# A decoder trunk in three-pass fp32r: up units as 512-column passes split around the products, a thirteenth Strassen block, and a pinned order for the first unit

## The chip, the cores and the metric

The kernel runs on one core of one Trainium2 chip. The metric is device time in microseconds of one execution; the time before is 938.76 us, the median of three runs (938.64 to 938.79). The core has five engines with a queue each: PE (TensorE, matrix products into PSUM), DVE (VectorE), ACT (ScalarE), POOL (GpSimd) and SP (SyncE), the last two here mostly issuing DMAs. Each queue runs in its own order; semaphores tie them together.

## The reference

Two decoder layers on 256 tokens of width 1024, in float32. Each layer has two sub-layers with a norm on both sides; the first has three branches (sliding-window attention, a gated recurrence, a causal pool), merged by gates. The change touches the second:

```python
mix = merged @ w_out[l]
h = h + rms_norm(mix, norm_mix_post[l])
m = rms_norm(h, norm_mlp_pre[l])
y = jnp.square(jax.nn.relu(m @ w_mlp_up[l])) @ w_mlp_down[l]     # 1024 -> 4096 -> 1024
h = h + rms_norm(y, norm_mlp_post[l])
```

and the start of the first layer, where the first 512 columns of the projection (keys and values) are computed from the normed input.

## The kernel before

**Products in three passes.** PE multiplies float32 operands in the type fp32r. To keep the precision, every operand is split into a high part (ScalarE writes a copy in fp32r, L99) and a low part (VectorE subtracts the copy, L100). A product is then high x high + high x low + low x high, three matmuls into the same PSUM bank (`mm3`, L106 to L109). Every weight passes through this: SP loads a unit of 128 x 1024 ("raw", seven buffers), ScalarE and VectorE make "wh" and "wl" (eight buffers each, shared with the other weight forms named below).

**Two forms of a product with the features on PSUM's free side.** `w_unit` (L373) makes one up unit: 256 hidden columns by 256 tokens, in two halves n of 128 hidden columns, each of 8 chunks x 3 matmuls with 256 moving columns, into one bank. `w_unit2`, used in the input projection, stores high and low features side by side, so that one matmul of 512 moving columns takes the weights' high part against both (L360), and a matmul of 256 takes the low part against the high features (L362); ScalarE copies the second half of the bank out, and VectorE adds the first half to it (`joined`).

**The block loop of the MLP** (`for j in range(nstr)`). The 4096 hidden columns make 16 blocks of 256. For the first 12 blocks the down product is done by Strassen's scheme: seven products (`down`, 21 matmuls) in place of eight (24 matmuls), accumulated over the blocks in seven PSUM banks of the eight. A block needs its weights in combined forms: "dh/dl" and "bh/bl" are splits of what the host laid out as differences, "sh/sl" are splits of two sums of weights. The sums of pairs ("dsum") are made in DRAM by accumulating DMAs (`make_sums`, issued at the steps SUM_AT of the first sub-layer); two further sums ("t") are made the same way for the blocks in FOUR, and by two VectorE adds (L917, L918) for the others. `hidden_forms` makes the forms of the hidden values ("sm", "xf"; L886 to L889). One round j of the loop: up unit j + 3 (the first round has two), forms for block j + 1, the seven products of block j. The last four blocks are plain (`plain`, 24 matmuls per block): block 12 alone, then 13 to 15 together (LAST), ordered by tokens and halves so that the norm behind can start early.

**The start.** PE runs six warm-up matmuls and three smaller ones (L136, L140). `first_features` transposes four chunks of the input at a time and writes their high and low parts, scaled by the gain; `kv_first` runs the key and value unit: four weight units, for each two token tiles of six matmuls, with the transposes of the other parts of the input placed between them. A scheduler orders each engine's instructions by when it thinks they can run, and by priority: `tc.high_priority` moves work ahead. The order on each queue is then fixed.

Of the kernel before, what the change touches and what calls it, by code (L numbers as in the profile page):

```python
# [18 lines left out]
T = 256  # L19
P = 128  # L20
# [6 lines left out]
WARM = (6, 3)  # L27
# [29 lines left out]

KV_ORDER = ((0, 0), (0, 1), (1, 0), (1, 1), (2, 0), (2, 1), (3, 0), (3, 1))
# [8 lines left out]
def trunk(ctx, tc, x, wts, rgw, par, gpost, eye, ctab, out):  # L67
# [28 lines left out]

    def split(hi, lo, src, scale=None):
        if scale is None:
            A.activation(hi, src, AF.Copy)  # L99
            V.tensor_tensor(out=lo, in0=src, in1=hi.bitcast(F32), op=ALU.subtract)  # L100
        else:
            A.activation(hi, src, AF.Copy, scale=scale)
            V.scalar_tensor_tensor(out=lo, in0=src, scalar=scale, in1=hi.bitcast(F32),
                                   op0=ALU.mult, op1=ALU.subtract)

    def mm3(o, lh, ll, rh, rl, start, stop, **kw):  # L106
        PE.matmul(o, lh, rh, start=start, stop=False, **kw)  # L107
        PE.matmul(o, lh, rl, start=False, stop=False, **kw)  # L108
        PE.matmul(o, ll, rh, start=False, stop=stop, **kw)  # L109
# [25 lines left out]
    for i in range(WARM[0]):  # L135
        PE.matmul(wps[:], warm[:, 0:P], warm[:], start=True, stop=True)  # L136

    def warm_up(n):
        for i in range(n):
            PE.matmul(wps[:, 0:256], warm[:, 0:P], idt[:].bitcast(BF16), start=True, stop=True)  # L140
# [49 lines left out]

    def split_to(n):
        while st["split"] < min(n, NHU):
            i = st["split"]
            load_to(i + 1)
            r = raw_t.pop(i)
            wh = his.tile([P, HU_COLS], F32R, tag="wh", name=f"wh{i}")
            wl = los.tile([P, HU_COLS], F32R, tag="wl", name=f"wl{i}")
            parts = 2 if i in fine else 1
            for k in range(parts):
                sl = slice(k * HU_COLS // parts, (k + 1) * HU_COLS // parts)  # L200
                split(wh[:, sl], wl[:, sl], r[:, sl])
            hu_t[i] = (wh, wl)
            st["split"] += 1
        load_to(n + NRAW - 1)
# [59 lines left out]
    def first_features(tt, part):  # L264

        tsl = slice(tt * P, (tt + 1) * P)
        ps = bank([P, 4, P])
        for c in range(4):
            PE.transpose(ps[:, c, :], h[:, tt, (4 * part + c) * P:(4 * part + c + 1) * P], ident)
        for c0 in (0, 2):  # L270
            for c in range(c0, c0 + 2):
                gain = prm[:, 0, PG_PRE + 4 * part + c:PG_PRE + 4 * part + c + 1]
                A.activation(uh[:, 4 * part + c, tsl], ps[:, c, :], AF.Copy, scale=gain)
                V.scalar_tensor_tensor(out=ul[:, 4 * part + c, tsl], in0=ps[:, c, :], scalar=gain,
                                       in1=uh[:, 4 * part + c, tsl].bitcast(F32), op0=ALU.mult, op1=ALU.subtract)
            yield

# [95 lines left out]
    def w_unit(hus, xh, xl):  # L373

        ps = bank([P, 2, T])
        for n in range(2):
            for i, (wh, wl) in enumerate(hus):
                a = wh.rearrange("p (k n) -> p k n", k=4)
                b = wl.rearrange("p (k n) -> p k n", k=4)
                for k in range(4):  # L380
                    c = 4 * i + k
                    mm3(ps[:, n, :], a[:, k, n * P:(n + 1) * P], b[:, k, n * P:(n + 1) * P],
                        xh[:, c, :], xl[:, c, :], c == 0, c == 7)
        return ps

    def s_hu(ps, hu, xh, xl, c0, tt, start, stop):
        wh, wl = hu
        a = wh.rearrange("p (k n) -> p k n", k=2)
        b = wl.rearrange("p (k n) -> p k n", k=2)
        for k in range(2):  # L390
            tsl = slice(tt * P, (tt + 1) * P)
            mm3(ps, xh[:, c0 + k, tsl], xl[:, c0 + k, tsl], a[:, k, :], b[:, k, :],
                start and k == 0, stop and k == 1)
# [53 lines left out]
    fa = first_features(0, 0)  # L447
    next(fa)
    warm_up(WARM[1])
    split_to(1)  # L450
    next(fa)
    load_to(CST)
    nc.sync.dma_start(cst[:], ctab)

    for l in range(L):
# [14 lines left out]
        def kv_first():  # L470

            pss = [bank([P, 512]) for _ in range(2)]
            for n, (i, tt) in enumerate(KV_ORDER):
                if tt == 0:
                    hk, = take(1)
                    hks.append(hk)
                s_hu(pss[tt][:], hks[i], uh, ul, 2 * i, tt, i == 0, i == 3)
                for t_, part in X_AFTER.get(n, ()):
                    hp(list)(first_features(t_, part))
# [390 lines left out]

        def up(j):
# [58 lines left out]
        def down(j, part):  # L930
            f = forms[j]
            w1, w4, w2, w3 = wforms[j]
            lo_, up_ = slice(0, 512), slice(512, 1024)

            for p, blk, w, cs in ((1, 2, w1, up_), (3, 6, w1, lo_), (2, 0, w4, lo_), (7, 5, w2, lo_), (5, 3, w2, up_),
                                  (6, 4, w3, lo_), (4, 1, w3, up_))[part]:
# [15 lines left out]
        for j in range(nstr):  # L952
            if j % 2 and j + 3 < nstr:
                load_sums(j + 3)
            for i in range(UPS[j]):
                up(nup)
# [6 lines left out]
                down(j, slice(0, 7) if UPS[j] == 1 else (slice(0, 4), slice(4, 7))[i])  # L963
# [30 lines left out]
        def last_rows(hus):  # L994
# [28 lines left out]
            V.tensor_tensor(out=rest[1][1][:], in0=tgt[1][1][:], in1=rest[1][1][:], op=ALU.add)  # L1023
# [10 lines left out]
        for j in range(nstr, NBLK - LAST):  # L1034
            if j not in hids:
                hidden_split(j)
            hus = take(2)
            ahead()
            for tt in range(2):
                for nh in range(2):  # L1040
                    if tgt[tt][nh] is None:
                        tgt[tt][nh] = bank([P, 512], nm="pr")
                    plain(j, hus, tt, nh)
            if j == nstr:
                rest = drain()
# [7 lines left out]
        for tt in range(2):  # L1053
# [3 lines left out]
            for nh in range(2):  # L1057
                for b in range(LAST):
# [50 lines left out]
def _layout(i):  # L1109
    qc = np.concatenate([np.arange(hd * 64, hd * 64 + 64) for hd in _HEADS])  # L1110
    units, rg, par, gp = [], [], [], []
    for l in range(L):
# [17 lines left out]
        up = _w_units(i["w_mlp_up"][l]).reshape(NBLK, 2, P, HU_COLS)  # L1130
# [47 lines left out]
```

## Time and profile before

| what | value |
|---|---|
| median of three runs | 938.76 us |
| the profiled execution | 938.37 us, of which the span on the core is 936.6 us |
| block loop and plain block 12, layer 0 (timeline of PE) | from 319.63 us, with ups 4 to 15; plain blocks from 446.34 us |
| splits of weights on VectorE (L100, wl) | 296 rows, 325.1 us |
| splits of weights on ScalarE (L99, wh) | 296 rows, 281.5 us |
| DMA | 217.30 MB, mean 232 GB/s |

How to read the profile: the page gives for each engine its busy time and share, then the span in 40 slices, the DMA queues, the chain of work that ended last (followed back from the last instruction to what released it), and groups of equal instructions with busy time and mean duration. A timeline row is: start in us, duration in us, engine, line, operation, what it writes <- what it reads, shape, count, and in brackets the idle time before it and who ended it. Matmuls overlap each other, so the time that one costs is the distance to the next start, not its duration.

### The profile page before, as it was taken

Reading aid. Unit: us, or ns where it says so; the run is one execution under the profiler, and the core shown is the slowest. Engines: PE = TensorE matmul, PEld = TensorE weight load, DVE = VectorE, ACT = ScalarE, POOL = GpSimd, SP = SyncE. Lnnn points to the kernel's source line nnn. Section 1 sums busy time; section 2 is a strip of 40 time slices with the busy share of each in tenths; the row PEclk is TensorE's granted clock in tenths of the full one; section 3 lists DMA queues with packets and bytes.
Section 4 is the critical chain, followed back from the end, with each engine's and each line's share of the span. In section 5 each row is a group of like instructions: output and inputs, shape, how many; then the busy total and the mean of one; then the engine's idle time right before and its main releaser. Section 6 shows DMA issues by size and latency. Waiting matters only on the chain.

```text
span 936.6 us, 14405 instructions
## 1 busy us (share of the span) xinstructions
PE 928.2 (99%) x5183; PEld 798.0 (85%) x5183; DVE 765.8 (82%) x1401; ACT 643.1 (69%) x1106; POOL 39.2 (4%) x44
## 2 busy tenths in 40 slices
PE   9999999999999999999999999999999999999997
PEld 6888977888888999999888888888888889999986
DVE  6978997989668798888786788788995597898884
ACT  7765765798637787677575665668894478777661
POOL 0001101001000000000000101010000000000000
PEclk9999999999999999999999999999999999999999
DMA  9898898968864767766469988978796467767631
GB/s 350 290 308 244 272 259 246 307 212 224 245 203 151 242 200 264 245 224 214 147 209 308 263 233 248 300 212 273 227 265 207 157 225 225 259 213 237 197 130 45
DMA packets 65496, 217.30 MB, mean 232 GB/s; under 512 B 7056, under 2 KB 7696, under 8 KB 65040
## 3 DMA queue, kind: packets, MB, share of 16 engines
q1 hardware_dynamic: 56160, 199.30, 61.0%
q0 software_dynamic: 8832, 16.78, 11.5%
q8 instruction: 40, 0.66, 0.3%
q14 instruction: 32, 0.26, 0.1%
q10 hardware_dynamic: 432, 0.30, 0.1%
HBM read 215.30 MB, written 34.60 MB: 267 GB/s over the span
## 4 chain that ended last, share of the span: by engine, by line
PE 99%; DMA 1%; DVE 0%; SPq 0%; ACT 0%; DVEq 0%; issue 0%
PE ps L107 18%; PE ps L109 18%; PE ps L108 18%; PE ps L360 9%; PE ps L400 7%; PE pr L107 6%; PE pr L108 6%; PE pr L109 6%; PE ps L362 5%; PE ps L534 1%; PE ps L582 1%; PE ps L571 1%; PE ps L283 1%; DMA h<-x 1%; PE ps L514 0%; PE ps L761 0%
## 5 line engine op out<-in xcount | busy, mean ns | idle before, releaser
L100 DVE TENSOR_TENSOR wl<-raw,wh 128x1024 fp32r<-128x1024 f32 (+1 forms) x296 | 325.1, 1120 | 61.9 <-ACT wh L99 52.5
L99 ACT ACTIVATE wh<-raw 128x1024 fp32r<-128x1024 f32 (+1 forms) x296 | 281.5, 983 | 116.3 <-PE ps L109 54.4
L107 PE MATMUL ps<-m,wh 128*128 128x256 f32 x448 | 126.8, 283 | 0.0
L109 PE MATMUL ps<-m,wl 128*128 128x256 f32 x448 | 126.8, 283 | 0.0
L108 PE MATMUL ps<-m,wh 128*128 128x256 f32 x448 | 126.8, 283 | 0.0
L360 PE MATMUL ps<-u,wh 128*128 128x512 f32 x384 | 96.9, 394 | 0.0
L107 PE MATMUL ps<-wh,u 128*128 128x512 f32 x224 | 87.7, 392 | 0.0
L109 PE MATMUL ps<-wh,u 128*128 128x512 f32 x224 | 87.4, 390 | 0.0
L108 PE MATMUL ps<-wl,u 128*128 128x512 f32 x224 | 87.4, 390 | 0.0
L108 PEld LDWEIGHTS ps<-m,wh 128*128 128x128 f32 x448 | 85.9, 192 | 1.0
L107 PEld LDWEIGHTS ps<-m,wh 128*128 128x128 f32 x448 | 85.9, 192 | 1.0
L109 PEld LDWEIGHTS ps<-m,wl 128*128 128x128 f32 x448 | 85.9, 192 | 0.0
L360 PEld LDWEIGHTS ps<-u,wh 128*128 128x128 f32 x384 | 69.4, 189 | 13.6 <-issue 0.7
L99 ACT ACTIVATE sh<-dsum 128x1024 fp32r<-128x1024 f32 x24 | 25.4, 1057 | 48.1 <-PE ps L108 48.1
L362 PEld LDWEIGHTS ps<-u,wl 128*128 128x128 f32 x384 | 52.4, 190 | 3.8
L362 PE MATMUL ps<-u,wl 128*128 128x256 f32 x384 | 53.5, 282 | 0.0
L107 PEld LDWEIGHTS ps<-wh,u 128*128 128x128 f32 x224 | 42.1, 188 | 9.7 <-issue 0.7
L109 PEld LDWEIGHTS ps<-wh,u 128*128 128x128 f32 x224 | 42.0, 188 | 8.8
L108 PEld LDWEIGHTS ps<-wl,u 128*128 128x128 f32 x224 | 42.1, 188 | 8.5 <-DVE wl L100 0.3
L169 POOL DMA_DIRECT2D sums<-wts x24 | 26.1, 1087 | 547.5 <-DMA sums<-wts 535.3
L100 DVE TENSOR_TENSOR sl<-dsum,sh 128x1024 fp32r<-128x1024 f32 x24 | 29.4, 1224 | 20.5 <-ACT sh L99 20.5
L553 ACT ACTIVATE pr<-ps,s 128x128 f32<-128x128 f32 (+1 forms) x64 | 25.9, 431 | 20.2 <-DVE s L544 20.2
(263 smaller groups left out, 2046.2 us busy)
## 6 DMA issues: line engine op xcount, KB each, us to landing
raw<-wts SPq DMA_DIRECT2D x291, 512.0 KB, 4.7
sums<-wts SPq DMA_DIRECT2D x24, 512.0 KB, 6.9
sums<-wts POOLq DMA_DIRECT2D x24, 512.0 KB, 8.6
dsum<-sums SPq DMA_DIRECT2D x12, 1024.0 KB, 6.4
raw<-wts SPq DMA_DIRECT2D x26, 256.0 KB, 3.5
sums<-wts SPq DMA_DIRECT2D x16, 256.0 KB, 6.9
sums<-sums POOLq DMA_DIRECT2D x16, 256.0 KB, 5.2
t<-sums SPq DMA_DIRECT2D x8, 512.0 KB, 4.4
```

Of the source, the lines that this page charges most:

```text
L99: A.activation(hi, src, AF.Copy)
L100: V.tensor_tensor(out=lo, in0=src, in1=hi.bitcast(F32), op=ALU.subtract)
L107: PE.matmul(o, lh, rh, start=start, stop=False, **kw)
L108: PE.matmul(o, lh, rl, start=False, stop=False, **kw)
L109: PE.matmul(o, ll, rh, start=False, stop=stop, **kw)
L169: nc.gpsimd.dma_start(t, u1[:, 0:512].unsqueeze(1).to_broadcast([P, 2, 512]), accum_op=ALU.add)
L283: PE.transpose(banks[c // 4][:, c % 4, :], src[c // 4][:, (c % 4) * P:(c % 4 + 1) * P], ident)
L360: PE.matmul(ps[:], ws[0][c], x2[:, :, c, :], start=c == 0, stop=False)
L362: PE.matmul(ps[:, 0, :], ws[1][c], x2[:, 0, c, :], start=False, stop=c == 7)
L400: PE.matmul(o, xx[:, c, tsl], ww[c], start=(n == 0 and c == 0), stop=(n == 2 and c == 7))
L534: PE.matmul(sc[hd // hp][:, hd % hp, :], qT[a, j // 2][rows, j % 2, blk * P:(blk + 1) * P], kTs[0][rows, a, 0:w], start=True, stop=True)
L553: A.activation(pr[:, j, :], sc[i][:, j, :], AF.Exp, bias=negm[:, hd:hd + 1], accum_out=sums[:, hd:hd + 1])
```

## The change

It has three parts.

1. In both layers, up units 5 to 15 (WIDE) take the form of `w_unit2`: `up_wide(j, n, hu)` makes one half n by eight matmuls of 512 columns and eight of 256, then a ScalarE copy, a VectorE add (both at high priority), relu and square. The first three of the block's seven products stand between the two halves, the other four behind the second. The host lays the up weights out so that a weight unit holds one half n whole; the old `w_unit` follows. The order of products 2 and 3 is exchanged.
2. 13 blocks go by Strassen's scheme, 3 are plain; every round has one up unit. FOUR has six blocks now, 0, 1 and 2 among them. The sums of pairs 10 to 12 are issued in rounds 0, 2 and 4 of the block loop (SUM_LATE).
3. Everything up to the end of the key and value unit keeps the order in which it is written (`pin`). The code there is written out step by step; `first_features` uses two banks of two chunks; small warm-up matmuls ("fill") stand between the first matmuls: 7 and 4 at the very start in place of 6 and 3, nine more in the first unit.

The core of the diff:

```diff
-WARM = (6, 3)
+WARM = (7, 4, (2, 0, 1, 3, 0, 0), 3)
-PLAIN = 4
+PLAIN = 3
-UPS = (2, 1, 1, 1, 1, 1, 1, 1, 1, 1, 1, 1)
+UPS = (1,) * 13
+WIDE = tuple(range(5, 16))
-SUM_AT = tuple(range(1, 25, 2))
-FOUR = (1, 4, 7, 10)
+SUM_AT = tuple(range(1, 21, 2))
+SUM_LATE = {3: 10, 5: 11, 7: 12}
+FOUR = (0, 1, 2, 4, 6, 8)
...
+    def pin(ins):
+        if pinned[0]:
+            tc.keep_in_program_order(ins)
...
+            unit(())
+            part(0, 0, WARM[2])
+            fb = first_features(1, 0)
+            next(fb)
+            warm_up(WARM[3])
+            next(fb)
+            unit((None, None, fb))
+            part(0, 1)
...
+        def up_wide(j, n, hu):
+            if n == 0:
+                zs[j] = ttile([P, 2, T], nm="z")
+            a, b = [w.rearrange("p (k n) -> p k n", k=8) for w in hu]
+            ps = bank([P, 2, T])
+            for c in range(8):
+                PE.matmul(ps[:], a[:, c, :], u2[:, :, c, :], start=c == 0, stop=False)
+            for c in range(8):
+                PE.matmul(ps[:, 0, :], b[:, c, :], u2[:, 0, c, :], start=False, stop=c == 7)
+            t = ttile([P, T], nm="jt")
+            with tc.high_priority(HP):
+                A.activation(t[:], ps[:, 1, :], AF.Copy)
+                V.tensor_tensor(out=t[:], in0=ps[:, 0, :], in1=t[:], op=ALU.add)
+            A.activation(t[:], t[:], AF.Relu)
+            A.activation(zs[j][:, n, :], t[:], AF.Square)
...
-                up(nup)
+                parts = slice(0, 7) if UPS[j] == 1 else (slice(0, 4), slice(4, 7))[i]
+                if nup in WIDE:
+                    hus = take(2)
+                    up_wide(nup, 0, hus[0])
+                    mid = parts.start + 3
+                    down(j, slice(parts.start, mid))
+                    up_wide(nup, 1, hus[1])
+                    parts = slice(mid, parts.stop)
+                else:
+                    up(nup)
+                if nup in SUM_LATE:
+                    make_sums(l, SUM_LATE[nup])
...
-        for j in range(nstr, NBLK - LAST):
...
+        rest = drain()
```

**PE in a round of the block loop.** Before, the last matmuls of an up unit (ps) and the first products (pr):

```order
L107 MATMUL ps<-m,wh_4127 128x256
L108 MATMUL ps<-m,wh_4127 128x256
L109 MATMUL ps<-m,wl_4128 128x256
L107 MATMUL pr<-dh,xf 128x512
L108 MATMUL pr<-dl,xf 128x512
```

Of the change, a whole first pass, three products, and the start of the second pass:

```order
L925 MATMUL ps<-m,wh_4062 128x512 x8
L927 MATMUL ps<-m,wl_4063 128x256 x8
L117 MATMUL pr<-dh,xf 128x512
L119 MATMUL pr<-dl,xf 128x512
L121 MATMUL pr<-dh,xf 128x512
L117 MATMUL pr<-bh,xf 128x512
L119 MATMUL pr<-bl,xf 128x512
L121 MATMUL pr<-bh,xf 128x512
L117 MATMUL pr<-dh,xf 128x512
L119 MATMUL pr<-dl,xf 128x512
L121 MATMUL pr<-dh,xf 128x512
L925 MATMUL ps<-m,wh_4066 128x512 x8
```

48 matmuls ahead of 21 have become 16, nine, 16 and twelve.

**VectorE in such a round**, where it makes the sums itself (t). Before:

```order
L100 TENSOR_TENSOR wl_4124<-raw_3991,wh_4123 128x1024
L100 TENSOR_TENSOR wl_4128<-raw_4011,wh_4127 128x1024
L100 TENSOR_TENSOR sl<-dsum,sh 128x1024
L100 TENSOR_TENSOR sl<-t_4100,sh 128x1024
L100 TENSOR_TENSOR bl<-raw_3897,bh 128x512
L886 TENSOR_TENSOR sm<-z 128x128
```

Of the change:

```order
L931 TENSOR_TENSOR jt<-ps,jt 128x256
L110 TENSOR_TENSOR wl_4401<-raw_4293,wh_4400 128x1024
L110 TENSOR_TENSOR sl<-dsum,sh 128x1024
L110 TENSOR_TENSOR sl<-t_4373,sh 128x1024
L110 TENSOR_TENSOR dl<-raw_4295,dh 128x1024
L931 TENSOR_TENSOR jt<-ps,jt 128x256
L110 TENSOR_TENSOR bl<-raw_4185,bh 128x512
L952 TENSOR_TENSOR sm<-z 128x128
```

Two adds (jt, L931) have come in, the first between two splits of up weights, the second behind the split of dl. ScalarE's rows around the second pass's copy (jt, L930), of the change:

```order
L109 ACTIVATE sh<-t_4373 128x1024
L109 ACTIVATE dh<-raw_4295 128x1024
L930 ACTIVATE jt<-ps 128x256
L109 ACTIVATE bh<-raw_4185 128x512
L109 ACTIVATE wh_4509<-raw_4384 128x1024
L932 ACTIVATE jt<-jt 128x256
```

The copy stands behind dh, and the relu (L932) two rows behind the copy.

**PE at the start**, from the first transposes of the input (h) on. Before:

```order
L107 MATMUL ps<-wh_136,u 128x512
L108 MATMUL ps<-wl_137,u 128x512
L269 MATMUL ps<-idt,h 128x128 x4
L109 MATMUL ps<-wh_136,u 128x512
L107 MATMUL ps<-wh_136,u 128x512
```

Of the change (buffer numbers kept; L153 are fills):

```order
L117 MATMUL ps_160<-wh0_135,u_114 128x512
L153 LDWEIGHTS warm_95
L153 MATMUL ps_99<-warm_95 128x256
L153 LDWEIGHTS warm_95
L153 MATMUL ps_99<-warm_95 128x256
L119 MATMUL ps_160<-wl0_136,u_114 128x512
L121 MATMUL ps_160<-wh0_135,u_114 128x512
L153 LDWEIGHTS warm_95
L153 MATMUL ps_99<-warm_95 128x256
L117 MATMUL ps_160<-wh0_135,u_114 128x512
```

The transposes of the second token tile (L288) have moved behind all six matmuls of the first unit, and fills have come between these. On VectorE the low parts of the features (u) stand there in another place too. Before:

```order
L100 TENSOR_TENSOR wl0_137<-raw0_116,wh0_136 128x512
L274 SCALAR_TENSOR_TENSOR u_113<-ps_124,prm_87,u_113 128x128
L100 TENSOR_TENSOR wl0_137<-raw0_116,wh0_136 128x512
L274 SCALAR_TENSOR_TENSOR u_113<-ps_124,prm_87,u_113 128x128
L274 SCALAR_TENSOR_TENSOR u_113<-ps_167,prm_87,u_113 128x128
```

Of the change:

```order
L110 TENSOR_TENSOR wl0_136<-raw0_117,wh0_135 128x512
L296 SCALAR_TENSOR_TENSOR u_114<-ps_125,prm_87,u_114 128x128 x2
L110 TENSOR_TENSOR wl0_136<-raw0_117,wh0_135 128x512
L296 SCALAR_TENSOR_TENSOR u_114<-ps_126,prm_87,u_114 128x128 x2
L296 SCALAR_TENSOR_TENSOR u_114<-ps_176,prm_87,u_114 128x128 x2
```

Two rows of u, not one, now stand ahead of the second half of wl0.

More of the change, by code (lines that the diff above doesn't have):

```diff
@@ L189, in load_to, with split_parts @@
             st["load"] += 1
+    def split_parts():
+        i = st["split"]
+        load_to(i + 1)
+        r = raw_t.pop(i)
+        wh = his.tile([P, HU_COLS], F32R, tag="wh", name=f"wh{i}")
+        wl = los.tile([P, HU_COLS], F32R, tag="wl", name=f"wl{i}")
+        hu_t[i] = (wh, wl)
+        st["split"] += 1
+        parts = 2 if i in fine else 1
+        for k in range(parts):
+            sl = slice(k * HU_COLS // parts, (k + 1) * HU_COLS // parts)
+            split(wh[:, sl], wl[:, sl], r[:, sl])
+            yield
     def split_to(n):
         while st["split"] < min(n, NHU):
[L193 to L203, printed above, removed]
+            list(split_parts())
         load_to(n + NRAW - 1)
@@ L392, in s_hu @@
             mm3(ps, xh[:, c0 + k, tsl], xl[:, c0 + k, tsl], a[:, k, :], b[:, k, :],
-                start and k == 0, stop and k == 1)
+                start and k == 0, stop and k == 1, fill=fill[3 * k:3 * k + 3])
     def by_pass(o, xh, xl, wh, wl, tt, mid=None):
@@ L472, in kv_first, with part, unit @@
             pss = [bank([P, 512]) for _ in range(2)]
[L473 to L479, printed above, removed]
+            def part(i, tt, *fill):
+                s_hu(pss[tt][:], hks[i], uh, ul, 2 * i, tt, i == 0, i == 3, *fill)
+            def unit(steps):
+                w = split_parts()
+                for f in steps:
+                    next(f if f else w, None)
+                hks.append(take(1)[0])
+            unit(())
[6 more added lines that the diff above has]
+            part(0, 1)
+            fa = first_features(0, 1)
+            next(fa)
+            part(1, 0)
+            fb = first_features(1, 1)
+            next(fb)
+            part(1, 1)
+            unit((fa, None, None, fa, fb))
+            part(2, 0)
+            part(2, 1)
+            unit((None, None, fb))
+            part(3, 0)
+            part(3, 1)
+            pinned[0] = False
             for tt in range(2):
```

93 lines of the change are left out of this document (46 added, 47 removed).

## The prediction

> **What bounds the kernel.** I read the page first: busy shares, the clock line, and the chain of work that ended last.
>
> ```profile
> span 936.6 us, 14405 instructions
> PE 928.2 (99%) x5183; PEld 798.0 (85%) x5183; DVE 765.8 (82%) x1401; ACT 643.1 (69%) x1106; POOL 39.2 (4%) x44
> PEclk9999999999999999999999999999999999999999
> PE 99%; DMA 1%; DVE 0%; SPq 0%; ACT 0%; DVEq 0%; issue 0%
> ```
>
> The chain is matrix work almost from end to end, and the granted clock shows no throttling. So a saved microsecond of PE is a microsecond of time, as long as nothing else becomes late. VectorE is the next engine, at 82% on average, but the average hides the stage that the change touches; there I look at one round.
>
> The timeline of PE gives the price of one round of the block loop in layer 0: an up unit of 48 matmuls, then 21 matmuls of seven Strassen products.
>
> ```profile
> 372.38 0.28 PE L107 MATMUL ps<-m,wh 128*128 128x256 f32 x1
> 372.49 0.28 PE L108 MATMUL ps<-m,wh 128*128 128x256 f32 x1
> ...
> 378.01 0.28 PE L109 MATMUL ps<-m,wl 128*128 128x256 f32 x1
> 378.13 0.40 PE L107 MATMUL pr<-dh,xf 128*128 128x512 f32 x1
> ...
> 380.21 0.39 PE L107 MATMUL pr<-sh,xf 128*128 128x512 f32 x1
> ...
> 382.96 0.28 PE L107 MATMUL ps<-m,wh 128*128 128x256 f32 x1
> ```
>
> Durations overlap, so I use starts. The up unit takes 378.13 - 372.38 = 5.75 us (0.12 per matmul of 256 columns), the seven products 382.96 - 378.13 = 4.83, their first three (nine matmuls) 380.21 - 378.13 = 2.08. A round is 10.58 us and PE never pauses in it.
>
> **Part 1, the wide up units.** The same arithmetic in another shape already stands in this kernel, in the input projection (L360, L362): eight matmuls of 512 columns with the weights' high part, eight of 256 with the low part. The chain of work shows four such passes back to back:
>
> ```profile
> 90.27 1.84 PE ps L360 x8
> 92.11 0.95 PE ps L362 x8
> 93.07 1.84 PE ps L360 x8
> 94.91 0.95 PE ps L362 x8
> 95.86 1.84 PE ps L360 x8
> ```
>
> Two passes, the work of one up unit, take 95.86 - 90.27 = 5.59 us, 5.58 by their durations. Eleven blocks (5 to 15) of each layer change: 22 x (5.75 - 5.58) = **3.7 us less**. The ups before block 5 keep the old form. Bounds 22 x 0.16 = 3.5 and 22 x 0.19 = 4.2, from the roundings of the starts.
>
> The Trainium skill speaks against this term ("TensorE: Matmul & The Clock Gate", section "Back-to-back issue gap"): a warm matmul starts N/2.4 + 2.5 ns after the last, so 109 ns for 256 columns and 216 for 512. By that, joining two of 256 saves 2.5 ns, and the 352 joined pairs 0.9 us, an estimate from the page's figures; the whole sum below would then be 1.8 us. The trace doesn't agree: its starts lie 0.12 and 0.23 us apart.
>
> **Part 2, the thirteenth Strassen block.** A plain block (block 12 in both layers) becomes seven products:
>
> ```profile
> 446.34 0.39 PE L107 MATMUL pr<-wh,hid 128*128 128x512 f32 x1
> ...
> 451.78 0.39 PE L107 MATMUL pr<-wh,hid 128*128 128x512 f32 x1
> ```
>
> Its 24 matmuls run from 446.34 to 451.78, 5.44 us. Against 4.83 that is 0.61 per layer, **1.2 us less**. The first round loses its second up, but the total of ups stays; that is order, not work.
>
> **Part 3, the first 20 us.** The timeline, PE and VectorE:
>
> ```profile
> 5.63 0.69 DVE L100 TENSOR_TENSOR wl<-raw,wh 128x512 fp32r<-128x512 f32 x1 [0.29 <-ACT wh L99]
> 5.91 0.50 PE L107 MATMUL ps<-wh,u 128*128 128x512 f32 x1
> 6.24 0.34 DVE L274 SCALAR_TENSOR_TENSOR u<-ps,prm,u 128x128 fp32r<-128x128 f32 x1
> 6.37 0.49 PE L108 MATMUL ps<-wl,u 128*128 128x512 f32 x1
> 6.50 0.68 DVE L100 TENSOR_TENSOR wl<-raw,wh 128x512 fp32r<-128x512 f32 x1
> 7.16 0.66 PE L269 MATMUL ps<-idt,h 128*128 128x128 f32 x4 [0.29 <-DMA h<-x]
> 9.74 0.60 PE L269 MATMUL ps<-idt,h 128*128 128x128 f32 x4
> 10.09 0.48 PE L109 MATMUL ps<-wh,u 128*128 128x512 f32 x1
> 19.03 0.39 PE L107 MATMUL ps<-wh,u 128*128 128x512 f32 x1
> ```
>
> The 48 matmuls of the key/value unit and 12 transposes lie between 5.91 and 19.03, 13.12 us. At 0.227 each (4.83 / 21 is 0.23) and 0.35 for four transposes (9.74 to 10.09) plus some 0.09 for the late weight load behind them, they need 12.2: PE waits 0.9 us, mostly at 6.37 to 7.16 for the second rows of h. The new order puts all six matmuls of the first unit ahead of those transposes. But then other data is late. VectorE now makes both low parts of the features before the second half of the weights' low part, so that half ends at 5.63 + 0.61 + 2 x 0.26 + 0.69 = 7.45, where it ended at 7.18. The fifth matmul starts at 7.5, the sixth ends at 7.95, the transposes at 8.3, and the next feature parts come off ScalarE at 8.65 and off VectorE at 9.1, which puts the end of the first unit at 10.1. Then 36 matmuls (8.17) and eight transposes (0.9 with the loads) remain: 19.2 against 19.03. The nine fill-in matmuls stand in just these waits, so they cost little and gain little. I take **0.2 us more**; bounds 0.9 less (all waits gone) and 1.1 more (nine fills at 0.12, the price of 256 columns above, none hidden).
>
> **Part 4, who must be in time in the block loop.** Seven product banks stand open, so one PSUM bank is left for every up pass. Before, ScalarE alone emptied it, in the 4.83 us of products. Now each pass is emptied by a ScalarE copy and a VectorE add, and after the first pass only three products, 2.08 us, cover that. The add stands in VectorE's queue, in order, behind the splits:
>
> ```profile
> 403.40 0.28 DVE L889 TENSOR_TENSOR sm<-z,sm 128x128 f32<-128x128 f32 x1
> 403.60 0.68 DVE L918 TENSOR_TENSOR t<-t,raw 128x512 f32<-128x512 f32 x1
> 404.20 1.22 DVE L100 TENSOR_TENSOR dl<-raw,dh 128x1024 fp32r<-128x1024 f32 x1
> 405.34 0.68 DVE L100 TENSOR_TENSOR xf<-sm,xf 128x512 fp32r<-128x512 f32 x1
> 405.94 0.55 DVE L100 TENSOR_TENSOR xf<-z,xf 128x384 fp32r<-128x384 f32 x1
> 406.41 2.35 DVE L100 TENSOR_TENSOR wl<-raw,wh 128x1024 fp32r<-128x1024 f32 x2
> ```
>
> The groups of instructions add mean durations (the number behind the busy time, in ns) of a ScalarE row of 1024 and of a copy and an add of 256 columns out of PSUM:
>
> ```profile
> L99 ACT ACTIVATE sh<-dsum 128x1024 fp32r<-128x1024 f32 x24 | 25.4, 1057 | 48.1 <-PE ps L108 48.1
> L368 ACT ACTIVATE xr<-ps 128x256 f32<-128x256 f32 x16 | 5.7, 392 | 0.0
> L369 DVE TENSOR_TENSOR xr<-ps,xr 128x256 f32<-128x256 f32 x16 | 6.4, 420 | 1.1 <-ACT xr L368 1.1
> ```
>
> By starts: 1.14 for 1024 columns, 0.60 for 512, 0.47 for 384, 0.20 for 128. A round in which VectorE forms the sums itself has five splits of 1024, four rows of 512, one of 384, four of 128: 9.4 us. Two adds bring 0.7 to 0.84 (starts and mean duration): **10.1 to 10.2 us against PE's new 5.58 + 4.83 = 10.41**. It fits, barely. In the rounds whose sums come by DMA it is 1.2 less.
>
> Now the place of the add. In the order of the change, ScalarE's row "dh" stands ahead of the second pass's copy; its buffer is freed by that pass's 512-column half, 0.95 before the pass's end, and a row of 1024 takes 1.06, so it ends 0.1 after the pass. Counted from that end: VectorE splits dl (to 1.3), adds (1.6), then does bl, sums, xf, wl and xf (0.60 + 0.80 + 1.20 + 0.47 + 1.14 + 0.60 = 4.8) and reaches the next first pass's add at 6.4. That pass ends at 2.75 + 2.79 = 5.54, the bank is due 2.08 later, at 7.62, and the add is done at 6.85. **Margin 0.8 us**; after the second pass it is 1.0. I charge nothing; if the cover goes, the rivals have the price. ScalarE's extra four short rows per round (about 0.8) lie in its idle 31%.
>
> At each layer's end the plain block no longer lies between the last up unit and the three last blocks. Those three need the last block's hidden values 2.75 + 2 x 1.36 + 0.45 = 5.9 after that unit; through copy, add, relu, square and split, behind two splits and the drains, VectorE has them at about 6.0 in layer 0, at 5 in layer 1. I take **0.1 more**, bounds 0 and 1.2 (one split more ahead). The transfers (two more pairs of sums by DMA per layer, those of pairs 10 to 12 made later) I charge with nothing: the late ones have five rounds until they are read, and DMA holds 1% of the chain, which the bounds cover.
>
> **Sum.** 3.7 + 1.2 - 0.2 - 0.1 = 4.6 us less. The profiled execution took 938.37 (span 936.6 and 1.8 around it): 933.8. The median of the runs shown is 938.76, 0.4 above it, so I say **934.2**. Its own range, from the bounds: 4.2 + 1.2 + 0.9 = 6.3 less, 932.5, to 3.5 + 1.2 - 1.1 - 1.2 = 2.4 less, 936.4.
>
> **Rivals.** (a) *The start gains.* If PE's waits go and no new ones come, 1.1 less than I say: 933.1. For it: the longest wait is plainly the order of the queue. Against it: the low parts come late.
>
> (b) *Columns are all that counts.* An up unit streams 48 x 256 = 12288 columns before and 16 x 512 + 16 x 256 after, the same. Then part 1 is nothing and the time is 938.76 - 1.2 + 0.3 = 937.9. Against it stand the starts above, 5.58 for 5.75. By the page's rule of part 1 it would lie near this.
>
> (c) *VectorE becomes the bound of its heavy rounds.* Seven rounds per layer form sums. If their VectorE work is 10.7 instead of 10.2, by waits on ScalarE before splits, PE waits 0.3 in 14 rounds, 4 us: 938.3.
>
> (d) *The last PSUM bank comes free too late* (slower). Same queue, worse: if VectorE's rows don't overlap at all, the round costs the sum of mean durations, 5 x 1.22 + 4 x 0.685 + 0.55 + 4 x 0.285 + 0.84 = 11.4, the first pass's add slips past its 2.08 us, and PE waits 1.0 in 14 rounds: 934.2 + 14 = 948. It decides for slower from 4.6 / 14 = 0.33 us of wait per heavy round. Against it: the rows do overlap in the trace, 404.20 to 405.34 for a 1.22.
>
> (e) *The change doesn't act*: no chance of its own, since PE's order holds the 512-column passes and one plain block less; only their price is open, and that is (b).
>
> **How the numbers follow.** Forecast 0.72, (a) 0.08, (b) 0.04, (c) 0.10, (d) 0.06. About 0.2% (1.9 us) is what a measurement of this kernel can tell from no change. Faster by more: the forecast, (a), and the better part of (c), 0.82; within it 0.12; slower 0.06. The range leaves out (b), (c) and (d), 0.20: from 932.6 to 936.6.
>
> **What would show it.** A PE round of 10.4 us in blocks 5 to 15 and starts of 0.23 in the up passes say part 1 is right; 10.58 says (b). PE waits named after the add's line, in front of an up pass, say (c) or (d). The query unit's first matmul at 19.2 says part 3 is right, 18.2 says (a). A wait before the last three blocks would be the layer's end. Wrong would be a stall in the mid stages: there the order of PE is unchanged, and I expect none.

## The result and the profile after

| | before | after |
|---|---|---|
| median of the runs | 938.77 us (6 runs, 938.64 to 941.19) | 934.12 us (6 runs, 934.07 to 935.13) |
| profiled execution | 938.37 us, span 936.6 | 934.13 us, span 932.4 |
| matmuls, PE busy | 5183, 928.2 us | 4836, 924.3 us |
| VectorE, ScalarE busy | 82%, 69% | 84%, 72% |

The ratio is 0.9944, with a 95% interval of 0.9934 to 0.9954. The forecast was 934.2, the range 932.6 to 936.6.

The page of the changed kernel, its span, its busy shares and the engines of the chain that ended last:

```profile
span 932.4 us, 13892 instructions
PE 924.3 (99%) x4836; PEld 778.8 (84%) x4836; DVE 780.7 (84%) x1454; ACT 668.6 (72%) x1200; POOL 48.2 (5%) x54
PE 99%; DMA 0%; DVE 0%; ACT 0%; issue 0%; DVEq 0%; SPq 0%
```

PE still bounds the whole. To find where the 4.2 us of span came from I cut both spans at the same points of the program: the query unit's first matmul, the first and the last product of layer 0, and the same two of layer 1. Each row of this view of the changed kernel is a stretch with its length and the busy time of PE, weight loads, VectorE, ScalarE and GpSimd in it, then the granted clock, the DMA share and GB/s.

```profile
0.00:19.73 19.73, 18.37 (x84) 12.88 (x85) 12.80 (x35) 14.61 (x37) 0.20 (x4) 1.00 0.90 340
19.73:320.28 300.55, 300.55 (x1594) 252.99 (x1592) 250.28 (x504) 208.64 (x376) 21.98 (x23) 1.00 0.80 251
320.28:467.48 147.20, 147.20 (x756) 125.40 (x755) 135.15 (x223) 118.45 (x207) 2.09 (x2) 1.00 0.72 244
467.48:779.23 311.75, 311.75 (x1645) 262.12 (x1645) 249.38 (x480) 214.01 (x392) 21.85 (x23) 1.00 0.77 243
779.23:925.66 146.43, 146.43 (x765) 125.40 (x763) 130.44 (x210) 111.95 (x188) 2.09 (x2) 1.00 0.64 217
```

The same view of the kernel before has 19.03, 300.60, 149.54, 311.86 and 148.86 us. The start is 0.70 longer, the two block loops with their ends are 2.34 and 2.43 shorter, the stretches between differ by 0.05 and 0.11. Sum: 4.23 less.

One round of the block loop after the change, on PE's timeline:

```profile
367.00 1.98 PE L925 MATMUL ps<-m,wh 128*128 128x512 f32 x8
368.81 1.12 PE L927 MATMUL ps<-m,wl 128*128 128x256 f32 x8
369.77 0.40 PE L117 MATMUL pr<-dh,xf 128*128 128x512 f32 x1
...
371.85 2.00 PE L925 MATMUL ps<-m,wh 128*128 128x512 f32 x8
373.69 1.11 PE L927 MATMUL ps<-m,wl 128*128 128x256 f32 x8
374.64 0.40 PE L117 MATMUL pr<-sh,xf 128*128 128x512 f32 x1
...
377.39 0.39 PE L925 MATMUL ps<-m,wh 128*128 128x512 f32 x1
```

The passes take 369.77 - 367.00 = 2.77 and 374.64 - 371.85 = 2.79, the round 377.39 - 367.00 = 10.39 instead of 10.58. VectorE's busy time in a round with sums of its own and in one without:

```profile
356.61:367.00 10.39, 10.39 (x54) 8.86 (x53) 10.13 (x17) 8.53 (x15) 1.04 (x1) 1.00 0.83 225
367.00:377.39 10.39, 10.39 (x55) 8.86 (x53) 9.01 (x15) 8.63 (x15) 0.00 (x0) 1.00 0.85 331
```

10.13 of 10.39 and 9.01 of 10.39: full, and not too full. The add on VectorE behind the first pass of the second of these rounds (its start and its length):

```profile
370.82 0.42 DVE L931 TENSOR_TENSOR jt<-ps,jt 128x256 f32<-128x256 f32 x1
```

The first pass ended at 369.77, the add at 370.82 + 0.42 = 371.24, and the second pass took the bank at 371.85: 0.6 to spare. In 17 of the 22 wide units the add ends 1.47 to 1.65 us after the first pass and 0.4 to 0.6 ahead of the second. In unit 6 it is late, here in layer 0, where the first pass ended at 348.83:

```profile
350.49 0.42 DVE L931 TENSOR_TENSOR jt<-ps,jt 128x256 f32<-128x256 f32 x1
...
350.96 2.13 PE L925 MATMUL ps<-m,wh 128*128 128x512 f32 x8
```

The add ends 2.07 us after the pass, the second pass starts 0.05 later than the three products alone would have it, and it takes 2.91 instead of 2.79. It is the same in layer 1. ScalarE has four rows of a norm (junk<-h, L319) in that stretch, from 343.80 to 345.13, and its copy starts 1.11 us after the pass instead of 0.59. These two rounds take 10.54 and 10.55 us instead of 10.39.

### The profile page after: what moved, and what is told of

Same layout as the page of the kernel before. It is cut to its first block, busy times and chain, and to the rows that moved or that the text cites. A ratio compares the mean times of both kernels' runs of the same rounds, so it can differ in the third digit from the quotient of the medians.

```text
span 932.4 us, 13892 instructions
## 1 busy us (share of the span) xinstructions
PE 924.3 (99%) x4836; PEld 778.8 (84%) x4836; DVE 780.7 (84%) x1454; ACT 668.6 (72%) x1200; POOL 48.2 (5%) x54
## 4 chain that ended last, share of the span: by engine, by line
PE 99%; DMA 0%; DVE 0%; ACT 0%; issue 0%; DVEq 0%; SPq 0%
PE ps L117 14%; PE ps L121 14%; PE ps L119 14%; PE ps L383 10%; PE ps L925 9%; PE ps L420 7%; PE pr L117 6%; PE pr L119 6%; PE pr L121 6%; PE ps L385 5%; PE ps L927 4%; PE ps L581 1%; PE ps L629 1%; PE ps L618 1%; PE ps L306 1%; PE ps L561 0%
## 5 line engine op out<-in xcount | busy, mean ns | idle before, releaser
L110 DVE TENSOR_TENSOR wl<-raw,wh 128x1024 fp32r<-128x1024 f32 (+1 forms) x292 | 320.8, 1116 | 60.6 <-ACT wh L109 52.4
L109 ACT ACTIVATE wh<-raw 128x1024 fp32r<-128x1024 f32 (+1 forms) x292 | 277.3, 982 | 120.6 <-PE ps L121 52.3
L925 PE MATMUL ps<-m,wh 128*128 128x512 f32 x352 | 87.6, 391 | 0.0
L925 PEld LDWEIGHTS ps<-m,wh 128*128 128x128 f32 x352 | 65.9, 188 | 14.4
L182 POOL DMA_DIRECT2D sums<-wts x26 | 29.9, 1149 | 585.7 <-DMA sums<-wts 546.0
L927 PEld LDWEIGHTS ps<-m,wl 128*128 128x128 f32 x352 | 48.0, 190 | 3.5
L927 PE MATMUL ps<-m,wl 128*128 128x256 f32 x352 | 49.1, 282 | 0.0
L117 PE MATMUL pr<-sh,xf 128*128 128x512 f32 x104 | 40.8, 392 | 0.0
L119 PE MATMUL pr<-sl,xf 128*128 128x512 f32 x104 | 40.7, 392 | 0.0
L121 PE MATMUL pr<-sh,xf 128*128 128x512 f32 x104 | 40.5, 389 | 0.0
L110 DVE TENSOR_TENSOR sl<-t,sh 128x1024 fp32r<-128x1024 f32 x26 | 31.8, 1222 | 9.7 <-ACT sh L109 9.7
```

What stands on the lines that cost most here:

```text
L109: pin(A.activation(hi, src, AF.Copy))
L110: pin(V.tensor_tensor(out=lo, in0=src, in1=hi.bitcast(F32), op=ALU.subtract))
L117: pin(PE.matmul(o, lh, rh, start=start, stop=False, **kw))
L119: pin(PE.matmul(o, lh, rl, start=False, stop=False, **kw))
L121: pin(PE.matmul(o, ll, rh, start=False, stop=stop, **kw))
L182: nc.gpsimd.dma_start(t, u1[:, 0:512].unsqueeze(1).to_broadcast([P, 2, 512]), accum_op=ALU.add)
```

## The experiments

The runs were made beside runs of the kernel before, whose median was 939.94, 940.20 and 938.93 on the three occasions, against 938.77 beside the changed kernel. So a run is judged by its ratio to the runs beside it and by its own stretches, not by its median alone. The fastest of these runs took 938.54 to 938.64 every time; the median moves with the share of runs at 940 to 942, and the ratio with it. So sizes of some tenths are read from the stretches. Stretches are cut as above, by the starts on PE's timeline.

### The up units narrow again

```diff
-WIDE = tuple(range(5, 16))
+WIDE = ()
```

> The changed kernel (934.1 us) with the eleven wide up units of each layer put back into 48 matmuls of 256 columns; the products again follow in one piece of seven, and the copy and add on the second half go. Theory of the prediction: each of the 22 units costs 5.75 us again where the changed kernel's trace has 5.56, so 22 x 0.17 to 22 x 0.19 = 3.7 to 4.2 more: 937.8 to 938.3, rounds of 10.58 us. Rival (b), only streamed columns count: 934.1, rounds of 10.4. Rival (c), the adds on VectorE cost something that the wide form hides: less than 3.7 more, for instance 936.

Measured: 937.91 us, ratio 0.9976 (0.9966 to 0.9986). The two block loops of this kernel:

```profile
320.48:469.54 149.06, 149.06 (x932) 134.75 (x931) 127.66 (x201) 107.32 (x162) 2.09 (x2) 1.00 0.70 241
781.37:929.72 148.35, 148.35 (x941) 134.73 (x939) 123.11 (x188) 100.71 (x144) 2.10 (x2) 1.00 0.62 213
```

Against the changed kernel 149.06 - 147.20 = 1.86 and 148.35 - 146.43 = 1.92 more, 3.78 in all: part 1's 3.7. Against the kernel before they are 0.48 and 0.51 shorter, 0.99 in all: what is left is the thirteenth block, with the sums that it needs. Rival (b) falls.

### Twelve Strassen blocks

```diff
-PLAIN = 3
+PLAIN = 4
-UPS = (1,) * 13
+UPS = (2,) + (1,) * 11
-SUM_LATE = {3: 10, 5: 11, 7: 12}
+SUM_LATE = {5: 10, 7: 11}
+        for j in range(nstr, NBLK - LAST):
...
+                    plain(j, hus, tt, nh)
```

> The changed kernel with block 12 a plain block again and twelve Strassen blocks. Theory of the prediction: 24 matmuls for 21 in each layer, 2 x 0.61 = 1.2 more, of which 0.1 may come back at the layer's end: 935.2 to 935.3. Rival, the saving was given back at the layer's end, since nothing lies between the last up unit and the three last blocks any more: 934.1.

This kernel leaves out one addition of 128 x 512 in the last layer, the last quarter of the plain block's product. Measured: 939.05 us, ratio 0.9991 (0.9982 to 1.0001), some 4 us above the first theory by the median, 2.7 by the ratio (0.9991 x 938.77 = 937.9). Layer 0's block loop took 152.10, 4.9 more than in the changed kernel; most of it is a stall, with a lower clock behind it (last section). ScalarE, VectorE and PE there:

```profile
360.52 1.06 ACT L109 ACTIVATE sh<-t 128x1024 fp32r<-128x1024 f32 x1 [3.04 <-DMA t<-sums]
361.49 1.04 ACT L109 ACTIVATE dh<-raw 128x1024 fp32r<-128x1024 f32 x1
362.44 0.36 ACT L930 ACTIVATE jt<-ps 128x256 f32<-128x256 f32 x1
```

```profile
361.62 1.23 DVE L110 TENSOR_TENSOR sl<-t,sh 128x1024 fp32r<-128x1024 f32 x1 [3.91 <-ACT sh L109]
362.76 1.22 DVE L110 TENSOR_TENSOR dl<-raw,dh 128x1024 fp32r<-128x1024 f32 x1
363.89 0.42 DVE L931 TENSOR_TENSOR jt<-ps,jt 128x256 f32<-128x256 f32 x1
```

```profile
362.06 0.39 PE L117 MATMUL pr<-dh,xf 128*128 128x512 f32 x1
364.37 2.70 PE L925 MATMUL ps<-m,wh 128*128 128x512 f32 x8 [1.92 <-DVE jt L931]
```

Read from the top: a transfer of the sums made by DMA lands 3.0 us after ScalarE is ready for it; ScalarE's row on it stands ahead of the copy, VectorE's ahead of the add; the last PSUM bank stays occupied, and PE waits 1.92 us. That is the mechanism of rival (d), but set off by a transfer and not by VectorE's load. So this run doesn't price the thirteenth block; a later one does.

### The start as before, and the start without fills

```diff
-WARM = (7, 4, (2, 0, 1, 3, 0, 0), 3)
+WARM = (6, 3)
-    pinned = [True]
+    pinned = [False]
...
```

> The changed kernel with the first unit, its features and the warm-up as before the change. The query unit's first matmul starts at 19.73 us in the changed kernel's trace and at 19.03 in the one before. Theory: those 0.70 us are the price of the new order and stay in the time to the end: 933.4. By the size in the prediction (0.2): 933.9. Rival, the later stages make them up, since they wait for nothing but the weights, which land at the same time: 934.1.

Measured: 934.80 us, ratio 0.9949 (0.9933 to 0.9966), between 933.89 and 938.38: not told apart by time. Its query unit starts at 19.50, where the old order had 19.03 in the kernel before. PE shows why:

```profile
6.23 0.50 PE L121 MATMUL ps<-wl,u 128*128 128x512 f32 x1
7.60 0.66 PE L289 MATMUL ps<-idt,h 128*128 128x128 f32 x4 [0.87 <-DMA h<-x]
```

In the old order PE waits for the second rows of h to land; they did at 7.12 in the kernel before and at 7.56 here, and the query unit followed 11.9 us later in both. In layer 1 this execution also lost 0.85 us, most of it in one round at the add again; ScalarE's row on a transferred sum started late there too, but what it waited for last was, by the trace, PE and not the transfer.

```diff
-WARM = (7, 4, (2, 0, 1, 3, 0, 0), 3)
+WARM = (7, 4, (0, 0, 0, 0, 0, 0), 0)
```

> The changed kernel without the nine matmuls on zeros in the first unit (6 between its matmuls, 3 behind the transposes of the second rows); the four before it stay. Theory of the prediction: they stand in waits, so nothing changes: 934.1, the query unit at 19.7. Rival, none hidden: 9 x 0.12 = 1.1 less, 933.0, at 18.6. Rival, they hold the clock up: the granted clock of the first 20 us falls and the time grows, by 0.3 or more.

Measured: 934.09 us, ratio 0.9938 (0.9925 to 0.9951); the query unit at 19.53, where the same order gives 19.55 to 20.37 with fills (below). So no cost of the fills is seen, nor that they keep the clock up.

### Less cover between the passes

```diff
-                    mid = parts.start + 3
+                    mid = parts.start + 2
```

> The changed kernel with two products instead of three between the two passes of a wide up unit, and five instead of four behind. Cover after the first pass: 1.39 us instead of 2.08. In the changed kernel's trace (367.00 to 371.85) that pass ends at 369.77 and the add that frees its PSUM bank ends at 371.15 to 371.24, 1.4 to 1.5 later. Theory (the bank is freed by an add that stands in VectorE's queue, margin 0.6 measured, 0.8 predicted): the margin is used up, waits of 0 to 0.1 in 22 units: 934.1 to 936.5. Rival, the bank is free as soon as a copy and an add can run (0.7 after the pass): nothing changes, 934.1. Rival, the add moves later with the queue: waits of 0.3 or more, 941 and above.

> The same with one product between the passes: cover 0.69 us. Theory: each of 22 units waits 1.45 - 0.69 = 0.75 for the add: 934.1 + 16.5 = 950.6, with PE waiting in front of the second pass on the add's line. Rival (copy and add run at once): 0.1 each at most, 934.1 to 936. Rival: the wait is longer than 0.75, because a longer pause also lowers the granted clock behind it: above 952.

In the second run the sum ends in + 1. Measured: 936.99 us with two products (ratio 0.9968, 0.9954 to 0.9981), 936.88 with one (0.9967, 0.9957 to 0.9978). Neither is the test it was meant to be. Here is PE with "one product" between the passes:

```profile
369.21 1.11 PE L927 MATMUL ps<-m,wl 128*128 128x256 f32 x8
370.16 0.40 PE L117 MATMUL pr<-dh,xf 128*128 128x512 f32 x1
...
372.49 0.39 PE L119 MATMUL pr<-sl,xf 128*128 128x512 f32 x1
372.72 2.01 PE L925 MATMUL ps<-m,wh 128*128 128x512 f32 x8
```

Eleven matmuls stand there and not three (five to eleven in the rounds of this run): the scheduler, which orders PE by when it thinks the bank will be free, moved products ahead of the second pass. So the cover was not the one that the edit names. The test was made again with PE's order held:

```diff
-                    mid = parts.start + 3
+                    mid = parts.start + 1
-                PE.matmul(ps[:], a[:, c, :], u2[:, :, c, :], start=c == 0, stop=False)
+                pe(PE.matmul(ps[:], a[:, c, :], u2[:, :, c, :], start=c == 0, stop=False))
...
+            tc.keep_in_program_order(ins)
```

> As the run with one product between the passes, but with PE's instructions of the block loop held in the written order (one product, then six), so that products can't be moved ahead of the waiting pass. Cover 0.69 us. Theory: the add that frees the bank ends 1.4 to 1.5 after the first pass, so PE waits 0.7 to 0.8 in each of 22 units, 15 to 18 us: 949 to 952. Rival (copy and add run as soon as the pass ends, 0.7 later): 934 to 936. Rival: the pauses lower the clock too: above 955.

Measured: 952.80 us, ratio 1.0146 (1.0132 to 1.0160), slower as the theory says. PE, VectorE, and PE's waits over the whole run:

```profile
405.92 0.40 PE L125 MATMUL pr<-dh,xf 128*128 128x512 f32 x1
...
407.27 2.11 PE L933 MATMUL ps<-m,wh 128*128 128x512 f32 x8 [0.50 <-DVE jt L939]
```

```profile
405.67 1.22 DVE L110 TENSOR_TENSOR wl<-raw,wh 128x1024 fp32r<-128x1024 f32 x1
406.80 0.42 DVE L939 TENSOR_TENSOR jt<-ps,jt 128x256 f32<-128x256 f32 x1
```

```profile
PE ps L933 <- DVE jt L939: 12.8, 22, 1.2
```

All 22 units wait for the add. The bank is free 407.27 - 405.92 = 1.35 us after the first pass (1.28 to 1.37 in most units). With the 2.08 us of three products that would leave 0.73. In the changed kernel itself, where the add meets other rows in its queue, 0.4 to 0.6 is left in most units (above). In unit 6 and in the last unit of each layer the bank came free 1.91 to 2.04 us after the pass here. By starts the 22 gaps grew by 16.4 us in all (1.35 for 0.69 in most), and the second pass takes 2.90 behind a pause instead of 2.79, 2.4 in all: together the 18.7 us. That is just above the theory's range; the clock has no part in it, it was 1.00 over both block loops. Nor is it the held order as such: a kernel with twelve blocks below holds it too, with three products between the passes, and takes 936.24.

### The sums on VectorE, and twelve blocks again

```diff
-FOUR = (0, 1, 2, 4, 6, 8)
+FOUR = (0,)
```

> The changed kernel with only block 0's second sums made by DMA; those of blocks 1, 2, 4, 6 and 8 are two VectorE rows of 512 (1.2 us by starts) in each such round instead, 10 rounds in all; 10 transfers of sums into SBUF and 20 within DRAM go. Theory of the prediction: a round with the sums on VectorE has 10.1 to 10.2 us of VectorE work and fits in PE's 10.39: 934.1. Rival (c), VectorE is the bound of such a round by waits on ScalarE: 0.3 in each of 10 more, 937. Third reading, from the traces: in rounds with the sums by DMA ScalarE waits for that transfer (0.3 to 0.9 us before 361.74 and 372.20), so taking them away frees margin, and the small wait of 0.2 in block 2's round (350.96) goes: 933.7.

Measured: 934.76 us, ratio 0.9948 (0.9934 to 0.9963). Two rounds that follow each other, both with sums on VectorE:

```profile
357.29:367.67 10.38, 10.38 (x55) 8.86 (x53) 10.38 (x19) 8.16 (x14) 1.05 (x1) 1.00 0.75 191
367.67:378.33 10.66, 10.66 (x55) 8.78 (x53) 10.14 (x17) 8.63 (x15) 0.00 (x0) 1.00 0.86 318
```

VectorE has work for 10.38 of 10.38 us in the first; the second, with 10.14, is the only round of its kind in layer 0 that lost as much as 0.28; there ScalarE waited 0.68 us for a transfer of raw weights (its wh row at 369.38), and the add came late behind it. The block loops are 0.29 and 0.02 longer than in the changed kernel (147.49 and 146.45). Ten more heavy rounds cost 0.3 in all, not 0.3 each: rival (c) falls. The third reading fails too, since nothing was gained.

The kernel with twelve blocks was then run with these sums and with PE's order held, its missing addition put back:

> The changed kernel with block 12 plain again and twelve Strassen blocks, PE's order in the block loop held as written (three products between the passes), and all sums but block 0's on VectorE, so that neither the moved products nor the late transfers of the first run with twelve blocks are there. Its fair neighbour is the run with the sums on VectorE. Theory: 0.6 more per layer, 1.2 in all, in the stretch from the first product to the last: 934.8 + 1.2 = 936.0. Rival: the thirteenth block gave nothing, 934.8.

Measured: 936.24 us, ratio 0.9968 (0.9957 to 0.9979), 1.5 above its neighbour by the medians, 1.4 by the fastest runs. Its block loops took 148.33 and 147.66, 0.84 and 1.21 more; in each layer some 0.4 of that is a new wait in one of the first rounds. So the thirteenth block is worth 0.4 to 0.8 per layer, with the predicted 0.61 between them.

### Wider still, and an earlier transpose

```diff
-WIDE = tuple(range(5, 16))
+WIDE = tuple(range(3, 16))
```

> The changed kernel with blocks 3 and 4 wide too, 4 more units in all. Theory: 4 x 0.19 (5.75 - 5.56) = 0.8 less, 933.4. Rival: in the first two rounds VectorE and ScalarE also carry the norm and the squares of the first blocks, so the add comes late and PE waits there: 934.1 or more.

Measured: 938.12 us, ratio 0.9985 (0.9976 to 0.9995): the rival was right that it costs. The scheduler again broke up passes and moved products, so it was run once more with the order held, together with block 2 wide and the transposes moved; before it, those two edits alone:

```diff
-            part(0, 0, WARM[2])
             fb = first_features(1, 0)
+            part(0, 0, (2, 0, 0, lambda: next(fb), 0, 0))
             next(fb)
-            warm_up(WARM[3])
-            next(fb)
-            unit((None, None, fb))
+            next(fb, None)
+            unit((None, None))
...
-        up(2)
+        for n, hu in enumerate(take(2)):
+            up_wide(2, n, hu)
```

> The changed kernel with two edits: the transposes of the second rows of h stand behind the fourth matmul instead of the sixth, in place of four fills, with their features ahead of the second weight unit; and block 2's up unit, before the loop, is wide. Theory on the start: in eight traces of the new order the query unit starts 11.5 to 11.7 us after these transposes, whatever landed when; they move from 7.9-8.8 to 7.2-8.3 (when h lands), so the query unit starts at 18.8 to 19.8 instead of 19.5 to 20.4: 0.6 less. On the up unit: 2 x 0.19 = 0.4 less. Together 933.1. Rival: the second weight unit's parts, now later on ScalarE and VectorE, take over: the query unit stays at 19.5 or later, 933.8.

Measured: 934.30 us, ratio 0.9949 (0.9936 to 0.9961): no gain over the changed kernel. The wide unit of block 2 did its part (5.56 us in both layers, 5.75 before). The start did not:

```profile
6.94 0.40 PE L117 MATMUL ps<-wh,u 128*128 128x512 f32 x1
8.06 0.66 PE L291 MATMUL ps<-idt,h 128*128 128x128 f32 x4 [0.72 <-DMA h<-x]
```

The transposes now wait for the landing, at 8.02 in this execution, and the query unit starts 11.7 us behind them, at 19.75. In layer 1 a transfer of sums came late again, and PE lost some 0.8 there:

```profile
832.48 1.06 ACT L109 ACTIVATE sh<-t 128x1024 fp32r<-128x1024 f32 x1 [1.62 <-DMA t<-sums]
```

> The same, with blocks 3 and 4 wide too and PE's order in the block loop held as written. Theory: the loss of the run with blocks 3 and 4 wide came from moved products, so held in order the 4 units give 4 x 0.19 = 0.8 less than the run before: 932.3. Rival: it came from ScalarE and VectorE, which carry the squares and the norm of the second rows in those rounds, so PE waits there whatever the order: 934 or more, with waits before the second passes of blocks 3 and 4.

Measured: 939.06 us, ratio 0.9999 (0.9990 to 1.0008). With the order held, PE waits in block 3's round, in front of products:

```profile
319.28 0.50 PE L125 MATMUL pr<-dh,xf 128*128 128x512 f32 x1 [0.17 <-ACT xf L109]
319.61 0.40 PE L127 MATMUL pr<-dl,xf 128*128 128x512 f32 x1
320.68 0.50 PE L129 MATMUL pr<-dh,xf 128*128 128x512 f32 x1 [0.67 <-DVE xf L110]
```

The first block's hidden forms (xf) are still being made when its products start only 2.9 us after the start of block 3's unit instead of 5.8; three products then take 3.79 us instead of 2.08 (4.20 in layer 1). So neither reading was whole: it is ScalarE and VectorE, but the products wait for their operands, not the pass for its bank. No version beat the changed kernel.

## Why the prediction was right

**Part 1, right.** Predicted 3.7 less, measured 3.78 by the narrow run. The pair of passes was priced from the input projection (5.58) and took 5.56. The formula of the Trainium skill ("TensorE: Matmul & The Clock Gate", section "Back-to-back issue gap"), which that section gives for a single matmul, would by my estimate have one joined pair save 2.5 ns. By the trace's starts it saves 2 x 0.120 - 0.227 us, 13 ns, and by the measured 3.78 us over 352 pairs 11 ns, four times what the formula gives.

**Part 2, right in kind, a little large.** Predicted 1.2 less and 0.1 back at the layer's end; measured 0.99 net between the kernel before and the narrow run. The layer's end itself, from the first matmul of the last three blocks, took 17.49 in layer 0 where it was 17.39 (451.78 to 469.17), and 16.71 in layer 1 both times.

**Part 3, right in sign, too small.** Predicted 0.2 more, measured 0.70. The step that failed is the one that put the end of the first unit at 10.1; it ended at 10.62, and from there to the query unit it took 9.11 (9.1 predicted). The fifth matmul starts at 7.54 (7.5), but the transposes start at 8.11, where an end at 8.3 asked for 7.95. Then ScalarE, VectorE and PE:

```profile
8.53 0.62 ACT L299 ACTIVATE u<-ps,prm 128x128 fp32r<-128x128 f32 x2 [1.25 <-PE ps L288]
```

```profile
9.18 0.61 DVE L296 SCALAR_TENSOR_TENSOR u<-ps,prm,u 128x128 fp32r<-128x128 f32 x2 [1.18 <-ACT u L299]
```

```profile
8.95 0.50 PE L117 MATMUL ps<-wh,u 128*128 128x512 f32 x1
...
10.62 0.60 PE L288 MATMUL ps<-idt,h 128*128 128x128 f32 x4
```

I had the first of VectorE's rows done at 9.1, alongside ScalarE's second; it only started at 9.18, right behind the end of ScalarE's pair (8.53 + 0.62 = 9.15). In the kernel before the two overlap, ScalarE first:

```profile
7.86 0.63 ACT L273 ACTIVATE u<-ps,prm 128x128 fp32r<-128x128 f32 x2 [0.88 <-PE ps L269]
...
8.26 0.61 DVE L274 SCALAR_TENSOR_TENSOR u<-ps,prm,u 128x128 fp32r<-128x128 f32 x2 [0.82 <-ACT u L273]
```

VectorE starts 0.40 us after ScalarE there, and 0.65 to 0.66 after it in each of the twelve traces with the new features. The old code writes the rows of the two engines by turns, the new one two of ScalarE's and then two of VectorE's. So half of the missing 0.5 came with this order of rows, which the forecast passed over; why VectorE then waits for both of ScalarE's rows the traces don't show. The size is not that of the order alone, though. In nine traces with the new order and its fills the query unit started between 19.55 and 20.37, in two with the old one at 19.03 and 19.50. In the old order it followed the landing of the second rows of h (issued at 2.12 every time, landed from 7.1 to 8.3); in the new one it followed their transposes, 11.6 to 11.7 later in every trace, and these stand behind the sixth matmul. One profiled execution can't tell a cost of 0.2 from one of 0.7; the means of the traces, 19.97 and 19.27, are 0.7 apart, but the second is a mean of two.

**Part 4, right about VectorE's load, too generous about the margin.** VectorE's round was predicted at 10.1 to 10.2 and took 10.13, and ten more heavy rounds cost 0.3 us in all. The margin at the last bank was predicted at 0.8, with the add done 6.85 - 5.54 = 1.31 us after the first pass. In most units it is done after 1.47 to 1.65, which leaves 0.4 to 0.6, and in unit 6 of each layer nothing is left, some 0.15 us each. My margin was worked out as if every round were alike, and as if ScalarE's queue held only work that was ready. The second of these is the larger hole. It is in the term that I charged with nothing "which the bounds cover": the transfers of the sums into SBUF. In the changed kernel's profiled execution they cost nothing. In two other kernels (twelve blocks, block 2 wide) ScalarE stood 3.0 and 1.6 us in front of one of them, and PE lost some 4 us and 0.8 in that stretch.

**The sum.** 3.78 + 0.99 - 0.70 and 0.16 in the other stretches make 4.23, against a predicted 4.6. The profiled execution took 934.13 (predicted 933.8). The range from the bounds was 932.5 to 936.4; the prediction does not say why it ends with 932.6 to 936.6 instead. The result lies in both. That the median came out within 0.1 of the forecast is partly chance: the start was 0.5 worse than I said, and the profiled execution of the kernel before lay 0.4 under its median, that of after on it.

## What to carry to other kernels

Price a new shape of matmul by the same shape elsewhere in the same trace, start to start; here that was right to 0.1 us in 3.8, and a column count or a rule for the gap was not. When a buffer is freed by an instruction in an in-order queue, list what stands ahead of it in the fullest round, not in a typical one, and ask of each row whether its input is surely there: a transfer that an engine waits for passes its lateness on to everything behind. To test such a margin hold the order of the waiting engine, or the scheduler will move the work and the test measures something else.

## What was not expected of the hardware

After the 1.9 us pause in the first run with twelve blocks, the granted clock (the figure before the last two) was down; two stretches of that run:

```profile
362.00:364.40 2.40, 0.48 (x3) 0.05 (x2) 2.40 (x4) 2.31 (x5) 0.00 (x0) 1.00 0.84 153
364.40:368.60 4.20, 4.20 (x17) 3.70 (x18) 4.20 (x10) 3.64 (x6) 0.00 (x0) 0.65 0.76 195
```

At 0.65 over 4.2 us some 1.5 us (0.35 x 4.2) went behind the pause, on top of the 1.9 in it. The drop did not come at once: the matmuls of 512 columns behind the pause start 0.23 us apart up to 365.6, and 0.43 apart from 366.0 on. The Trainium skill ("TensorE: Matmul & The Clock Gate", section "What's actually happening") puts the drop behind an idle window of about 3.4 us; this one came behind 1.9 us without a matmul. The pauses with one product between the passes, 22 of up to 1.2 us, left it at 1.00.

For how long the first matmuls ran at half pace differed between executions. The four fills at 5 us in the changed kernel, and the same four in the run with the sums on VectorE:

```profile
5.04 0.60 PE L153 MATMUL ps<-warm 128*128 128x256 bf16 x4
```

```profile
5.10 1.06 PE L153 MATMUL ps<-warm 128*128 128x256 bf16 x4
```

They start 0.11 us apart in the first and 0.21 in the second. In the second, h had landed early (7.2), but the transposes of its second rows started at 8.70 instead of 8.11, and the query unit at 20.35.
